# Up- and down-projection on eight named PSUM banks, two recombination steps at higher priority, and adding transfers behind the scaling

## The chip, the cores and the metric

The kernel runs as one program on 1 core of a Trainium2 chip. The metric is the time of one execution in microseconds on the device. Five engines work at the same time, each through its own instructions in order: TensorE (PE) multiplies matrices and writes into PSUM, VectorE (DVE), ScalarE (ACT) and GpSimd (POOL) do elementwise work, and SyncE (SP) issues most of the DMA transfers. An engine waits for another only by a semaphore on the instruction that needs it. PSUM, in which matmuls accumulate, is used here as eight banks, each of which holds one tile of 128 x 512 float32.

## The reference

One decoder layer on x of 1024 tokens by 1024 channels in float32. Cut to what matters:

```python
def conv_ffn(xn, w_up, conv_w, conv_b, w_down):
    u = xn @ w_up                                   # 1024 x 5632
    upad = jnp.pad(u, ((0, 0), (CONV_WIDTH - 1, 0), (0, 0)))
    c = conv_b
    for j in range(CONV_WIDTH):                     # CONV_WIDTH = 3
        c = c + upad[:, j:j + S] * conv_w[j]
    gate, val = jnp.split(c, 2, axis=-1)            # 2816 each
    return (jax.nn.silu(gate) * val) @ w_down

def reference(x, ...):
    xn = rmsnorm(x, norm_mix_w)
    da_q, da_k, da_v, sw_q, sw_k, sw_v, g_da, g_sw = split_cols(xn @ w_in)
    ...
    y_da = diff_attention(da_q, da_k, da_v, lam, lam_init, subln_w)
    y_sw = sliding_window_attention(sw_q, sw_k, sw_v, sinks)
    merged = sigmoid(g_da) * (y_da @ w_br_da) + sigmoid(g_sw) * (y_sw @ w_br_sw)
    x = x + merged @ w_mix_out
    x = x + conv_ffn(rmsnorm(x, norm_ffn_w), w_up, conv_w, conv_b, w_down)
    return rmsnorm(x, norm_final_w)
```

## The kernel before

The stages follow each other: the projection with w_in (up to about 235 us of the profiled execution), attention (to about 490 us), the gates and the mixing product (to about 664 us), the up-projection (`hidden`, to about 1093 us), the down-projection (`down`) with the final norm (from 1100 us to the end). Data lie transposed, channels over the 128 partitions and tokens along them, in two halves of 512 tokens.

The large products are made by the Strassen-Winograd scheme. A pair of output column blocks (128 channels each) over two halves of tokens is a 2 x 2 block matrix, and seven products P1 to P7 of sums and differences replace eight. Each operand is also split in a high part and a low part (`wh`, `wl` for weights, `sh`, `sl` for their sums), where ACT casts the high part and DVE subtracts it from the raw value to get the low one; three matmuls (high x high, high x low, low x high) stand for one. So a product is 12 matmuls of 128 x 128 by 512, and one pair is 84.

In the up-projection the loop runs over j = 0 to 21, and pair j is made of columns j and j + 22 of w_up (gate and value). PE makes the products of a pair in the order P1, P2, P5, P6, P7, P3, P4 (for the last pair P1, P2, P5, P6, P7, P4, P3), each into a tile of its own in PSUM. Around them, per pair:

- POOL makes the sums of weight blocks (lines 156 to 159: `sa`, `sb` from `raw` and `rv`), from which ACT casts `sh` and DVE makes `sl` (line 172).
- `recombine` makes the four blocks of the result from the seven products. ACT copies P1 into s1 (line 524). DVE then reads the other products out of PSUM: line 526 takes P2, line 527 takes P6 into u2, line 528 takes P7 into u3 = u2 with P7, lines 529 and 530 take P5, line 532 takes P3 and line 533 P4. A bank is free again when the steps that read it are done.
- `conv` and `glu` of the pair before (j - 1): POOL and DVE scale the two column tiles `us` (line 1254), ACT starts the convolution (line 1268), DVE does its other two taps (lines 1270 and 1271, once for each of the two tiles), ACT applies silu (line 1243), DVE multiplies gate and value (line 1246), and the result goes to DRAM (`hd`), from which the down-projection reads it again.

What sets the order: the code is written pair after pair, and a scheduler places each engine's instructions by priority and readiness on a model; `high_priority` moves what it encloses ahead by as many places, `issue_after` keeps an instruction behind another one. On the chip each engine's order is fixed.

PSUM: in `hidden` a pool `psF` of eight tiles hands a bank to each product as it is asked for. In `down` another pool `psD` has four tiles named `d` and four named `y`, on the same eight banks: a chain of accumulating products in `down` (one output block m) has one of them. The first chains are y with m = 0 to 3 on stage P1, each with k chunks 0 to 5: 18 matmuls each (line 1324), weights `wh` and `wl` of a chain made by lines 191 (ACT) and 193 (DVE) from a load of w_down (line 181). Their other operand, the high and low parts of `hd` tiles 0 to 5, is made at the end of `hidden` (lines 897 and 898, in tiles named `sh`, `sl`, `rv`).

In the projection, pairs of w_in columns go the same way, by the same `recombine`; afterwards POOL multiplies the two column tiles `us` by the norm factor (line 514). In that stage there also go transfers to DRAM that prepare sums of other weights for later stages (`presum`): a copy (line 126, issued by SP), and a transfer that adds to what is there (line 128, `accum_op`), which POOL issues, so that it stands in POOL's queue among its elementwise work. Their results, `md` and `ud`, are read by the mixing product and by the first pairs of the up-projection.

Of the kernel before, what the change touches and what calls it, by code (L numbers as in the profile page):

```python
# [17 lines left out]
P = 128  # L18
# [4 lines left out]
H2 = 512  # L23
# [26 lines left out]
class Trunk:  # L50
# [270 lines left out]
    def project(self):  # L321
# [6 lines left out]
        with ExitStack() as ctx:  # L328
# [170 lines left out]
            for j, ms in enumerate(self.pairs):  # L499
                w = self.next_w()  # L500
                for c in SUMS[j]:
                    with tc.issue_after(self.sync), tc.issue_after(self.sum):
                        self.presum(*c)
# [6 lines left out]
                for m, u in zip(ms, us):  # L510
                    if self.kind[m] == "g":
                        nc.sync.dma_start(self.gd[m - 18], u)
                    else:
                        nc.gpsimd.tensor_tensor(u, u, self.rstd, ALU.mult)
                        self.keep(m, u, (tp, "hi"))
        self.uw = None

    def recombine(self, ps, us, tp, o, after=None, pre=False):
# [8 lines left out]
        tt(u2, ps["P6"], s1, sub(pre))  # L527
        tt(u3, u2, ps["P7"], sub(pre))
# [571 lines left out]
    def hidden(self, w0):  # L1100
        nc, tc = self.nc, self.tc
        with self.hctx as ctx:
            e = ctx.enter_context
            psF = e(tc.tile_pool(name="psF", bufs=8, space=PSUM, reuse_waits="tile"))
            self.psT = psF
# [4 lines left out]
            for j in range(NF):  # L1110
                w, ps = ready.pop(j) if j else (w0, {})
                if j == 0:
# [8 lines left out]
                    ssq = self.tl(psF, [P, H2], "t")  # L1121
                    self.col_sums(ssq, [self.rstd[:, H2:]], 4, 4)
                    for i in (1, 6):
                        name, a, b = prods[i]
                        ps[name] = self.tl(psF, [P, H2], "t")
# [13 lines left out]
                for name, a, b in (prods[i] for i in ((0, 1, 2, 5, 3, 6, 4) if j == NF - 1 else (0, 1, 2, 5, 3, 4, 6) if j else range(7))):  # L1139
                    if name not in ps:  # L1140
                        ps[name] = self.tl(psF, [P, H2], "t")
# [13 lines left out]
                with nullcontext() if j else tc.issue_after(self.ms):  # L1155
                    self.recombine(ps, us, tp, 2, self.lo.ins if j == NF - 1 else None, j < NPRE)
                if j < NF - 1:
# [12 lines left out]
                    for name, a, b in prods[:2 if j == 0 else 0]:  # L1170
                        ps[name] = self.tl(psF, [P, H2], "t")
                        self.product(ps[name], w[a], b)
                if j == 0:
                    for hf in range(2):
                        sp = self.tl(psF, [P, H2], "t")
                        self.spread(sp, rs, hf * 4)
                        nc.scalar.copy(self.rstd[:, hf * H2:(hf + 1) * H2], sp)
                if j > NF - 3:
                    self.front = None

                self.us = us
                for w in range(2):
# [3 lines left out]
                    else:  # L1186
                        self.defer.append(f)

# [85 lines left out]
    def down(self):  # L1274

        nc, tc = self.nc, self.tc
        with ExitStack() as ctx:
            e = ctx.enter_context
            psD = self.psD = e(tc.tile_pool(name="psD", bufs=4, space=PSUM, reuse_waits="tile"))
# [4 lines left out]
            bank = lambda n: self.tl(psD, [P, H2], "dy"[n])  # L1284
# [60 lines left out]
            for stage in STAGES:  # L1345
                which, start, o, hf, done = plan[stage]
                for c in range(2):
                    for m in range(4):
# [5 lines left out]
                        if start and c == 0:  # L1354
                            chains[which][m] = bank(which)
# [156 lines left out]
```

## Time and profile before

| | us |
|---|---|
| median of 3 runs (lowest, highest) | 1326.28 (1325.94, 1328.66) |
| the profiled execution | 1327.68 |
| its span | 1325.7 |
| mean granted TensorE clock of it | 0.995 of full speed |
| PE busy, share of the span | 1302.1, 98% |
| DVE busy, share | 1075.4, 81% |
| ACT busy, share | 635.2, 48% |
| POOL busy, share | 498.0, 38% |

The profiled execution took 1.4 us more than the median, and 2.0 us of it lie outside its span. The shares are means over stages that differ: PE and DVE stand close to each other in the up-projection and far apart elsewhere. In the rows of the profile a group is named by line, engine, operation and tiles (out<-in), and an idle time is put down to the instruction that ended last of those waited for.

### The profile page before, as it was taken

The page shows a single profiled execution, that of the slowest core. Times are in us where ns is not written, and L with a number is a line of the kernel's source. Part 1 is how long each engine was busy: PE and PEld are TensorE (multiplying, and loading weights), DVE is VectorE, ACT ScalarE, POOL GpSimd, SP SyncE. Part 2 cuts the span into 40 slices and gives each one's busy share as a digit, 9 for nine tenths or more (in the row PEclk, how much of TensorE's full clock was granted, in tenths as well). Part 3 has the DMA queues.
Part 4 walks back from the last instruction along what each step waited for, and adds up shares of the span by engine and source line. Part 5 has one row for each costly group of instructions (what it writes and reads, how often), then busy time and mean ns, then how long its engine had stood idle before and what let it go on. Part 6 is the DMA issues. An engine that isn't in the chain of part 4 may idle for free.

```text
span 1325.7 us, 17315 instructions
## 1 busy us (share of the span) xinstructions
PE 1302.1 (98%) x6162; PEld 1081.6 (82%) x6162; DVE 1075.4 (81%) x1516; ACT 635.2 (48%) x1010; POOL 498.0 (38%) x399
## 2 busy tenths in 40 slices
PE   9999999999999999999999999999999997999997
PEld 7887888888888878888888788878888886888886
DVE  8835865289888977667899999999999997896865
ACT  9422232276667764335764343333434344554543
POOL 0456665000011015743327567766766632000002
PEclk9999999999999999999999999999999998999999
DMA  8366887876552256569763336554635227953534
GB/s 308 124 171 198 231 220 231 255 194 176 151 145 78 69 186 217 165 196 256 211 209 136 120 135 167 152 182 139 202 100 155 72 76 262 335 175 118 164 97 147
DMA packets 85510, 229.57 MB, mean 173 GB/s; under 512 B 9520, under 2 KB 17328, under 8 KB 85168
## 3 DMA queue, kind: packets, MB, share of 16 engines
q1 hardware_dynamic: 63328, 187.04, 42.5%
q0 software_dynamic: 9216, 24.12, 10.9%
q10 hardware_dynamic: 12880, 17.31, 3.7%
q8 instruction: 48, 0.79, 0.3%
q14 instruction: 38, 0.31, 0.1%
HBM read 173.39 MB, written 84.41 MB: 194 GB/s over the span
## 4 chain that ended last, share of the span: by engine, by line
PE 64%; DVE 17%; issue 9%; DMA 4%; POOL 4%; ACT 2%; SPq 0%; POOLq 0%; DVEq 0%; ACTq 0%
PE t L1097 13%; PE y L1324 9%; PE d L1324 7%; PE m L1059 6%; PE g L212 4%; PE g L213 4%; PE g L214 4%; DVE wl L172 3%; DVE c L1270 3%; PE sc L700 3%; DMA rv<-in_w_up 2%; DVE c L1271 2%; POOL sf L156 1%; DVE c L1246 1%; PE t L716 1%
## 5 line engine op out<-in xcount | busy, mean ns | idle before, releaser
L193 DVE TENSOR_TENSOR wl<-raw,wh 128x1024 fp32r<-128x1024 f32 (+2 forms) x91 | 109.7, 1207 | 52.5 <-ACT wh L191 42.7
L191 ACT CAST wh<-raw 128x1024 fp32r<-128x1024 f32 (+2 forms) x91 | 80.4, 885 | 105.5 <-PE y L1324 52.8
L1254 POOL TENSOR_TENSOR us<-us,rstd 128x1024 f32<-128x1024 f32 x42 | 93.5, 2301 | 57.3 <-DVE us L532 29.0
L1268 ACT ACTIVATE c<-us,vecs 128x1024 f32<-128x1024 f32 x44 | 54.7, 1247 | 114.0 <-POOL us L1254 109.9
L229 POOL TENSOR_TENSOR rs<-ms,mhalf 128x8 f32<-128x8 f32 (+2 forms) x9 | 13.3, 1476 | 236.4 <-DVE ms L227 230.2
L156 POOL TENSOR_TENSOR sf<-rv 128x512 f32<-128x512 f32 x29 | 59.8, 2061 | 104.6 <-DMA rv<-in_w_up 49.8
L172 DVE TENSOR_TENSOR sl<-sf,sh 128x1024 fp32r<-128x1024 f32 x58 | 74.0, 1276 | 10.8 <-ACT sh L170 10.7
L1097 PE MATMUL t<-x,wh 128*128 128x512 f32 x240 | 79.8, 390 | 0.0
L170 ACT CAST sh<-sf 128x1024 fp32r<-128x1024 f32 x58 | 60.0, 1042 | 39.2 <-POOL us L1253 19.7
L172 DVE TENSOR_TENSOR wl<-raw,wh 128x1024 fp32r<-128x1024 f32 x29 | 69.7, 2404 | 4.0 <-ACT wh L170 3.9
L1271 DVE SCALAR_TENSOR_TENSOR c<-us,vecs,c 128x1024 f32<-128x1024 f32 x44 | 72.7, 1685 | 0.1
L212 PE MATMUL g<-xh,wh 128*128 128x512 f32 x176 | 71.1, 404 | 0.9 <-ACT g L629 0.8
L1097 PE MATMUL t<-x,sh 128*128 128x512 f32 x220 | 70.8, 390 | 0.0
L214 PE MATMUL g<-xh,wl 128*128 128x512 f32 x176 | 70.5, 401 | 0.0
L213 PE MATMUL g<-x,wh 128*128 128x512 f32 x176 | 70.4, 400 | 0.0
L1270 DVE SCALAR_TENSOR_TENSOR c<-us,vecs,c 128x1024 f32<-128x1024 f32 x44 | 67.1, 1559 | 1.2 <-ACT c L1268 1.2
L158 POOL TENSOR_TENSOR sf<-raw,rv 128x512 f32<-128x512 f32 x29 | 53.1, 1830 | 34.4 <-DVE sl L172 34.4
L1324 PE MATMUL y<-h,wh 128*128 128x512 f32 (+1 forms) x224 | 65.3, 375 | 0.0
L704 DVE CUSTOM_DVE_ANT_0 L<-sc,bias 128x128 f32<-128x128 f32 (+7 forms) x64 | 47.8, 752 | 16.7 <-PE sc L700 13.7
L683 POOL MEMSET aT<- 128x128 f32 x32 | 6.1, 204 | 145.8 <-PE t L729 97.8
L1097 PE MATMUL t<-z,sh 128*128 128x512 f32 x176 | 55.7, 398 | 4.0 <-DVE u L527 4.0
L705 ACT ACTIVATE L<-L,sm 128x128 f32<-128x128 f32 (+7 forms) x64 | 49.6, 778 | 20.0 <-DVE sm L704 17.4
(350 smaller groups left out, 4097.1 us busy)
## 6 DMA issues: line engine op xcount, KB each, us to landing
u<-qd SPq DMA_DIRECT2D x70, 256.0 KB, 6.5
raw<-in_w_in SPq DMA_DIRECT2D x22, 512.0 KB, 6.3
raw<-in_w_up SPq DMA_DIRECT2D x22, 512.0 KB, 5.3
hd<-c SPq DMA_DIRECT2D x22, 512.0 KB, 2.6
sdP<-in_w_down POOLq DMA_DIRECT2D x16, 704.0 KB, 8.5
rv<-in_w_up SPq DMA_DIRECT2D x20, 512.0 KB, 3.7
hc<-hd SPq DMA_DIRECT2D x33, 256.0 KB, 4.8
gr<-gd SPq DMA_DIRECT2D x16, 512.0 KB, 4.4
```

The lines of the kernel that those rows point to most:

```text
L172: low = nc.vector.tensor_tensor(lo, src, hi.bitcast(F32), ALU.subtract)
L191: self.hi = nc.scalar.copy(wh, raw)
L193: self.lo = (eng or nc.vector).tensor_tensor(wl, raw, wh.bitcast(F32), ALU.subtract)
L212: nc.tensor.matmul(ps, wh[:, kc + o, :], ah, start=first and n == 0, stop=False)
L213: nc.tensor.matmul(ps, wh[:, kc + o, :], al, start=False, stop=False)
L214: nc.tensor.matmul(ps, wl[:, kc + o, :], ah, start=False, stop=last and n == len(kcs) - 1)
L1059: nc.tensor.matmul(ps, v[:, m % 2 * 4 + k, :], x, start=start and k == j == 0, stop=k == 3 and j == 2, skip_group_check=True)
L1097: nc.tensor.matmul(ps, (ah, ah, al)[p][:, k, :], (bh, bl, bh)[p], start=first and n == p == 0, stop=last and p == 2 and n == len(ks) - 1, ...
L1254: i = (nc.vector if m % NF == 0 else nc.gpsimd).tensor_tensor(us[:, 2:], us[:, 2:], self.rstd, ALU.mult)
L1270: nc.vector.scalar_tensor_tensor(c, us[:, 1:T + 1], cw[1], c, ALU.mult, ALU.add)
L1271: nc.vector.scalar_tensor_tensor(c, us[:, 0:T], cw[0], c, ALU.mult, ALU.add)
L1324: nc.tensor.matmul(ps, v[:, k - k0, :], x, start=start and k == i == 0, stop=k == HK - 1 and i == 2, skip_group_check=True)
```

## The change

There are three edits.

1. One PSUM pool, `psF`, is now used by `hidden` and `down`, with eight tiles that are named by number. A table (`banks`) says for each pair which product has which bank. From j = 2 on, P1 takes the bank that stood free, P2 the one that P1 had, P5 that of P2, P6 and P7 keep theirs, P3 takes that of P5 and P4 that of P3 (for the last pair P3 and P4 change places), and the bank of P4 becomes the free one. The chains of `down` then take fixed banks: y with m = 0 the free bank, m = 1 to 3 those of P1, P6 and P7 of the last pair; the d chains those of P2, P5, P4 and P3. `last_norm` gets its banks by name.
2. In `recombine` the steps u2 and u3 (before: lines 527 and 528) are put at a priority that is higher by 150 for the pairs 1 to 20 of the up-projection.
3. In the projection, the transfers of `presum` are put behind the scaling of the pair's last column tile instead of behind the weight sums.

```diff
@@ project
             for j, ms in enumerate(self.pairs):
                 w = self.next_w()
-                for c in SUMS[j]:
-                    with tc.issue_after(self.sync), tc.issue_after(self.sum):
-                        self.presum(*c)
...
                     else:
-                        nc.gpsimd.tensor_tensor(u, u, self.rstd, ALU.mult)
+                        last = nc.gpsimd.tensor_tensor(u, u, self.rstd, ALU.mult).ins
                         self.keep(m, u, (tp, "hi"))
+                for c in SUMS[j]:
+                    with tc.issue_after(self.sync), tc.issue_after(last):
+                        self.presum(*c)
@@ recombine
-        tt(u2, ps["P6"], s1, sub(pre))
-        tt(u3, u2, ps["P7"], sub(pre))
+        with self.tc.high_priority(early):
+            tt(u2, ps["P6"], s1, sub(pre))
+            tt(u3, u2, ps["P7"], sub(pre))
@@ hidden
-            psF = e(tc.tile_pool(name="psF", bufs=8, space=PSUM, reuse_waits="tile"))
-            self.psT = psF
+            self.psF = self.fctx.enter_context(tc.tile_pool(name="psF", bufs=1, space=PSUM, reuse_waits="tile"))
+            banks = dict(P1=0, P5=1, P3=2, P7=3, P6=4, P2=6, P4=7)
...
+                if j == 1:
+                    banks, free = dict(P1=0, P2=5, P5=1, P6=2, P7=7, P3=6, P4=4), 3
+                elif j:
+                    b = banks
+                    c, d = ("P4", "P3") if j == NF - 1 else ("P3", "P4")
+                    banks = {"P1": free, "P2": b["P1"], "P5": b["P2"], "P6": b["P6"], "P7": b["P7"], c: b["P5"], d: b["P3"]}
+                    free = b["P4"]
...
-                        ps[name] = self.tl(psF, [P, H2], "t")
+                        ps[name] = self.bank(banks[name])
...
-                    self.recombine(ps, us, tp, 2, self.lo.ins if j == NF - 1 else None, j < NPRE)
+                    self.recombine(ps, us, tp, 2, self.lo.ins if j == NF - 1 else None, j < NPRE, 150 if 0 < j < NF - 1 else 0)
...
+                if j == NF - 1:
+                    self.ybanks = [free] + [banks[n] for n in ("P1", "P6", "P7")]
+                    self.dbanks = [banks[n] for n in ("P2", "P5", "P4", "P3")]
...
+    def bank(self, n):
+        return self.tl(self.psF, [P, H2], f"t{n}")
@@ down
-            psD = self.psD = e(tc.tile_pool(name="psD", bufs=4, space=PSUM, reuse_waits="tile"))
...
-            bank = lambda n: self.tl(psD, [P, H2], "dy"[n])
...
-                            chains[which][m] = bank(which)
+                            chains[which][m] = self.bank((self.dbanks, self.ybanks)[which][m])
...
-    def last_norm(self, psD, sqs, x3, t0, a, b, pieces):
+    def last_norm(self, banks, sqs, x3, t0, a, b, pieces):
```

How the order of instructions changes is shown at three places. Numbers behind a tile's name tell copies apart; what stands in brackets is whom an instruction waits for.

**DVE, one pair in the middle of the up-projection.** `wl` is the low part of the next weights, `c` are the tiles of the convolution, `sl` the low part of weight sums, `u2` and `u3` the two steps of `recombine`, `t` a product in PSUM. Before:

```order
L172 TENSOR_TENSOR wl_1316_7550<-raw_1311_7538,wh_1315_7548 128x1024
L1270 SCALAR_TENSOR_TENSOR c_1323_7568<-us_1305_7524,vecs_80,c_1323_7568 128x1024
L1270 SCALAR_TENSOR_TENSOR c_1324_7574<-us_1306_7525,vecs_80,c_1324_7574 128x1024
L1271 SCALAR_TENSOR_TENSOR c_1323_7568<-us_1305_7524,vecs_80,c_1323_7568 128x1024
L1271 SCALAR_TENSOR_TENSOR c_1324_7574<-us_1306_7525,vecs_80,c_1324_7574 128x1024
L172 TENSOR_TENSOR sl_1320_7558<-sf_1314_7543,sh_1319_7556 128x1024
L1246 TENSOR_TENSOR c_1323_7568<-c_1323_7568,c_1324_7574 128x1024
L527 TENSOR_TENSOR u2_1335_7675<-t_1328_7620,s1_1334_7674 128x512
L528 TENSOR_TENSOR u3_1336_7676<-u2_1335_7675,t_1329_7633 128x512
```

After (lines 1284, 1285 and 1260 are lines 1270, 1271 and 1246 of before, and 528 to 530 are 527 to 529):

```order
L172 TENSOR_TENSOR wl_1316_7550<-raw_1311_7538,wh_1315_7548 128x1024
L1284 SCALAR_TENSOR_TENSOR c_1323_7568<-us_1305_7524,vecs_80,c_1323_7568 128x1024
L1284 SCALAR_TENSOR_TENSOR c_1324_7574<-us_1306_7525,vecs_80,c_1324_7574 128x1024
L1285 SCALAR_TENSOR_TENSOR c_1323_7568<-us_1305_7524,vecs_80,c_1323_7568 128x1024
L528 TENSOR_TENSOR u2_1335_7675<-t2_1328_7620,s1_1334_7674 128x512
L1285 SCALAR_TENSOR_TENSOR c_1324_7574<-us_1306_7525,vecs_80,c_1324_7574 128x1024
L172 TENSOR_TENSOR sl_1320_7558<-sf_1314_7543,sh_1319_7556 128x1024
L529 TENSOR_TENSOR u3_1336_7676<-u2_1335_7675,t7_1329_7633 128x512
L1260 TENSOR_TENSOR c_1323_7568<-c_1323_7568,c_1324_7574 128x1024
```

u2 has moved ahead of the second of the two last taps, and u3 ahead of the product of gate and value. This is so for j = 1 to 20; the last pair has the order of before.

**PE, from the last matmuls of the up-projection to the first of the down-projection.** `t_1710` (`t1_1710`) is the last product, P3 of j = 21; `y_1726` (`t6_1726`) is the first chain of `down`. Before:

```order
L1097 MATMUL t_1710_9725<-B22_3_5762,sh_1670_9476 128x512 x2
L1097 MATMUL t_1710_9725<-B22_3_5762,sl_1671_9478 128x512
L1324 MATMUL y_1726_9795<-sh_1698_9629,wh_1690_9606 128x512 [waits DVE_49,Activation_49]
L1324 MATMUL y_1726_9795<-sh_1698_9629,wh_1690_9606 128x512
L1324 MATMUL y_1726_9795<-sh_1698_9629,wl_1691_9608 128x512
L1324 MATMUL y_1726_9795<-sl_1699_9632,wh_1690_9606 128x512 x2
```

After:

```order
L1098 MATMUL t1_1710_9725<-B22_3_5762,sh_1670_9476 128x512 x2
L1098 MATMUL t1_1710_9725<-B22_3_5762,sl_1671_9478 128x512
L1336 MATMUL t6_1726_9791<-sh_1698_9629,wh_1690_9606 128x512 [waits Activation_49]
L1336 MATMUL t6_1726_9791<-sh_1698_9629,wh_1690_9606 128x512
L1336 MATMUL t6_1726_9791<-sh_1698_9629,wl_1691_9608 128x512 [waits DVE_49]
L1336 MATMUL t6_1726_9791<-sl_1699_9632,wh_1690_9606 128x512 x2
```

The matmuls and their order are the same. The first matmul of the chain waited for DVE and ACT, and waits for ACT alone now; the third, which reads `wl`, has a wait for DVE that it had no need of before. The chain's tile is bank 6, that of P4 of j = 20.

**POOL, in the projection, behind the weight sums of one pair.** `us` are the two column tiles, `sf` the weight sums, `ud` and `mdP5` the results of `presum`. Before:

```order
L158 TENSOR_TENSOR sf_129_939<-raw_126_934,rv_127_936 128x512
L159 TENSOR_TENSOR sf_129_939<-raw_126_934,sf_128_938 128x512
L128 DMA ud0_92<-in_w_up 128x512
L514 TENSOR_TENSOR us_120_913<-us_120_913,rstd_83 128x1024
L128 DMA ud1_93<-in_w_up 128x512
L156 TENSOR_TENSOR sf_154_1083<-rv_153_1081 128x512
```

After:

```order
L158 TENSOR_TENSOR sf_129_939<-raw_126_934,rv_127_936 128x512
L159 TENSOR_TENSOR sf_129_939<-raw_126_934,sf_128_938 128x512
L511 TENSOR_TENSOR us_120_907<-us_120_907,rstd_83 128x1024
L128 DMA mdP5_88<-in_w_mix 128x512 x4
L156 TENSOR_TENSOR sf_154_1083<-rv_153_1081 128x512
```

The scaling of the second column tile now follows the weight sums at once, and a pair's adding transfers follow behind it. The same holds for the other pairs, and those of the first pair are issued one pair later than before. On SP, the copies of `presum` move a place or two with them, and at the start of `down` some of the weight loads come a few places earlier among the loads of `hd`.

More of the change, by code (lines that the diff above doesn't have):

```diff
@@ L1124, in hidden @@
                         name, a, b = prods[i]
-                        ps[name] = self.tl(psF, [P, H2], "t")
+                        ps[name] = self.bank(banks[name])
                         self.product(ps[name], w[a], b)
@@ L1140, in hidden @@
                     if name not in ps:
-                        ps[name] = self.tl(psF, [P, H2], "t")
+                        ps[name] = self.bank(banks[name])
                         self.product(ps[name], w[a], b, low=name == "P1")
```

20 lines of the change are left out of this document (10 added, 10 removed).

## The prediction

> **What bounds the kernel now.** First the page's busy shares, then the chain of waits grouped for PE.
>
> ```profile
> PE 1302.1 (98%) x6162; PEld 1081.6 (82%) x6162; DVE 1075.4 (81%) x1516; ACT 635.2 (48%) x1010; POOL 498.0 (38%) x399
> ```
>
> ```profile
> PE y L1324 <- DVE us L532: 7.1, 1, 7.1
> PE t L1097 <- DVE u L527: 4.0, 5, 1.6
> PE t L1097 <- DVE wl L172: 0.8, 1, 0.8
> ```
>
> PE is the bound; 23.6 us of the span are not busy. Of the waits, three kinds touch the change: one of 7.1 us in which the first chain of the down-projection stands for line 532, five in which P6 stands for line 527, and one of 0.8 us for `wl` in the projection: 11.9 us together. Next, PE at the boundary of up and down, in order of time:
>
> ```profile
> 1093.01 0.39 PE L1097 MATMUL t<-B,sl 128*128 128x512 f32 x1
> 1100.51 1.19 PE L1324 MATMUL y<-sh,wh 128*128 128x512 f32 x2 [7.12 <-DVE us L532]
> 1104.49 0.82 PE L1324 MATMUL y<-rv,wh 128*128 128x512 f32 x2
> 1106.75 0.62 PE L1324 MATMUL y<-sh,wh 128*128 128x512 f32 x2
> 1110.83 0.62 PE L1324 MATMUL y<-sh,wh 128*128 128x512 f32 x2
> ```
>
> From 1106.75 to 1110.83 is one chain of 18 matmuls: 4.08 us, 0.227 each. The chain before it took 6.24 us, because its first nine matmuls (1100.51 to 1104.49) went at 0.44 each: the stop cost 7.12 us and then 9 x 0.215 = 1.9 us of slow matmuls. Last, the up-projection by windows, one pair each, from line 527 to line 527, under a row for 17 pairs:
>
> ```profile
> 734.21:1062.44 328.23, 325.11 (x1425) 266.74 (x1426) 322.12 (x273) 127.83 (x136) 217.24 (x153) 1.00 0.48 144
> 753.35:772.49 19.14, 19.14 (x86) 15.71 (x85) 19.00 (x17) 7.49 (x8) 11.73 (x9) 1.00 0.44 158
> 791.64:808.71 17.07, 17.07 (x77) 13.98 (x76) 16.93 (x18) 6.03 (x6) 12.04 (x8) 1.00 0.68 178
> 808.71:830.61 21.90, 21.90 (x98) 17.94 (x96) 20.83 (x17) 9.07 (x10) 16.53 (x14) 1.00 0.53 138
> ```
>
> The columns behind the time are PE, weight load, DVE, ACT and POOL. 84 matmuls at 0.227 are 19.04 us. DVE is busy for 19.00 of 19.14 us and over the 17 pairs for 98%; the mean pair takes 328.23 / 17 = 19.31. So in this stage DVE sets the pace, by 0.1 us in regular pairs and more in irregular ones (17.07 then 21.90, together 38.97 against 38.28 for two regular).
>
> **The change, part by part.** *Banks.* Within the up-projection the plan is the one the old pool arrived at (P6 and P7 in their own banks, the others in rotation), so nothing moves there. At the boundary the first chain no longer needs the bank of the last product. What is late next is read from DVE and ACT, whose order here stays:
>
> ```profile
> 1092.32 0.95 DVE L193 TENSOR_TENSOR wl<-raw,wh 128x768 fp32r<-128x768 f32 x1
> 1096.91 1.06 DVE L193 TENSOR_TENSOR wl<-raw,wh 128x768 fp32r<-128x768 f32 x1
> 1099.68 0.68 DVE L532 TENSOR_TENSOR us<-t,u 128x512 f32<-128x512 f32 x1
> 1100.28 1.27 DVE L1271 SCALAR_TENSOR_TENSOR c<-us,vecs,c 128x1024 f32<-128x1024 f32 x1
> 1107.59 0.96 DVE L193 TENSOR_TENSOR wl<-raw,wh 128x768 fp32r<-128x768 f32 x1 [6.04 <-ACT wh L191]
> ```
>
> ```profile
> 1097.19 1.24 ACT L1268 ACTIVATE c<-us,vecs 128x1024 f32<-128x1024 f32 x1 [2.53 <-POOL us L1254]
> 1106.72 0.84 ACT L191 CAST wh<-raw 128x768 fp32r<-128x768 f32 x1 [8.29 <-PE y L1324]
> ```
>
> On DVE's clock: chain 0 follows at 1093.24; its `wl` is done at 1093.27 and is read by the third matmul only, at 1093.7. It ends at 1097.32. Chain 1 reads its `wl` (done at 1097.97) in its third matmul, due at 1097.77: 0.2 late, so it ends at 1101.6. Chain 2 has its `wh` cast when chain 0 is read (1097.3), but ACT is in line 1268 until 1098.4: cast until 1099.3, in time. Its `wl` stands behind line 1271 (end 1101.55), so 1102.5 against 1102.05: 0.45 late. Chain 2 thus runs as if begun at 1102.05, where it began at 1110.83: **8.8 us** gained. The stops that are left are under half a microsecond; stops of up to 1.6 us in the up-projection (the waits above) left the granted clock at 1.00 in the windows above, so I count no slow matmuls.
>
> *Loads of the down-projection.* Does the rest follow 8.8 us earlier?
>
> ```profile
> 1099.78 9.13 SPq L181 DMA_DIRECT2D raw<-in_w_down  x2
> ```
>
> ```profile
> 1104.00:1109.00 5.00, 5.00 (x21) 4.05 (x20) 1.41 (x2) 1.88 (x3) 0.00 (x0) 0.91 0.03 13
> 1109.00:1165.00 56.00, 56.00 (x248) 46.39 (x247) 49.99 (x66) 31.83 (x49) 4.76 (x2) 1.00 0.96 327
> ```
>
> SP stands at the second of two loads until about 1108.6, when the `wl` of chain 2 has read its `raw`; DMA is idle (0.03) until then and afterwards 0.96 full for 56 us. That `wl` now ends at 1102.5 instead of 1108.55, so the loads begin 6.0 us earlier, 2.8 less than PE. PE never waited in those 56 us, so there is slack, of a size that the trace does not show. Bounds 0 and 2.8 us; I take 0.5, near the lower end, since no wait of PE stands there now.
>
> *u2 and u3 earlier.* No instruction is added; two move on DVE. DVE now, with POOL beside it:
>
> ```profile
> 766.79 3.51 DVE L1271 SCALAR_TENSOR_TENSOR c<-us,vecs,c 128x1024 f32<-128x1024 f32 x2
> 770.22 1.21 DVE L172 TENSOR_TENSOR sl<-sf,sh 128x1024 fp32r<-128x1024 f32 x1
> 771.36 1.21 DVE L1246 TENSOR_TENSOR c<-c,c 128x1024 f32<-128x1024 f32 x1
> 772.49 0.68 DVE L527 TENSOR_TENSOR u<-t,s 128x512 f32<-128x512 f32 x1
> 773.28 0.69 DVE L528 TENSOR_TENSOR u<-u,t 128x512 f32<-128x512 f32 x1
> 774.00 0.69 DVE L529 TENSOR_TENSOR us<-u,t 128x512 f32<-128x512 f32 x1
> 774.60 0.68 DVE L530 TENSOR_TENSOR u<-u,t 128x512 f32<-128x512 f32 x1
> ```
>
> ```profile
> 771.51 2.21 POOL L158 TENSOR_TENSOR sf<-raw,rv 128x512 f32<-128x512 f32 x1 [2.19 <-DVE sl L172]
> 773.68 1.30 POOL L159 TENSOR_TENSOR sf<-raw,sf 128x512 f32<-128x512 f32 x1
> ```
>
> Line 527, 528 and 529 hang on each other and start 0.79 and 0.72 apart where independent ones are 0.60 apart (529 and 530 do not hang on each other): spread out, that gives back 0.3 us a pair. Against it: line 158 runs 1.30 us when alone (as line 159 does), but 2.21 here, because it stood until line 1246 was done; both work on SBUF alone, while 527 to 530 read PSUM and were not slowed by POOL. Now u3 stands between `sl` and 1246. Line 158, released by `sl`, starts under u3 (0.6 us), and 1246 stands for the other 1.30 - 0.6 = 0.7 us. So a regular pair costs +0.7 - 0.3 = +0.4. The irregular pairs come from here:
>
> ```profile
> 804.04 2.47 DVE L1271 SCALAR_TENSOR_TENSOR c<-us,vecs,c 128x1024 f32<-128x1024 f32 x2
> 816.00 5.56 DVE L172 TENSOR_TENSOR wl<-raw,wh 128x1024 fp32r<-128x1024 f32 x1
> 805.37 4.57 POOL L156 TENSOR_TENSOR sf<-rv 128x512 f32<-128x512 f32 x1 [4.72 <-DMA rv<-in_w_up]
> ```
>
> `rv` landed late, line 156 then stood behind four DVE operations in a row until line 527, its successors piled up, and DVE's `wl` paid with 5.56 instead of 1.2 us. With u2 between the two runs of line 1271, POOL gets its turn earlier; I give each double pair -0.5, between nothing and -1.0 (its whole excess, 38.97 - 38.28 = 0.7, and 0.3 for the spacing). Of the 17 pairs, (328.23 - 17 x 19.14) / 0.7 = 4 are double, 9 regular; over the 20 pairs that is 10.6 regular and 4.7 double: 10.6 x 0.4 - 4.7 x 0.5 = **+1.9 us** on DVE, which PE follows. The 4.0 us of waits for line 527 are no gain of their own: u2 releases P6 some 3.5 us earlier (the rows of 1271, `sl` and 1246 above), but P4 then waits for the `wl` of A22, which DVE makes in the same lap.
>
> The Trainium skill (SBUF — State Buffer, Who interferes with whom) says that a DVE instruction with two SBUF inputs and a GpSimd instruction that reads SBUF share an exclusive lock, and whichever issues first holds it while the other fully blocks. By that rule 1246 pays the 0.7 us in every pair, as taken above; line 156 at 805.37, which stood while DVE started two more such operations, shows that the first to ask is not always the first to get it, and if DVE kept its turn here too, the sum would be -0.3 a pair, the third rival below.
>
> *Projection.* The scaling on POOL stood behind an adding transfer:
>
> ```profile
> 115.51 0.82 POOL L128 DMA_DIRECT2D ud<-in_w_up  x1
> 116.08 2.67 POOL L514 TENSOR_TENSOR us<-us,rstd 128x1024 f32<-128x1024 f32 x1
> 118.78 1.06 ACT L545 ACTIVATE hi<-us 128x1024 fp32r<-128x1024 f32 x1 [12.88 <-POOL us L514]
> ```
>
> The scaling now starts 116.08 - 115.51 = 0.57 us earlier; from it hang ACT's `hi`, the casts behind that, and the `wl` that PE waited 0.84 us for. Bounds 0 and 0.57, I take **0.4**. The transfers go out up to one pair later; their results are read from about 550 us on, which covers a delay of some 20 to 30 us; SP's copies hide behind its idle time.
>
> *Sum* against the profiled 1327.68: 8.8 + 0.4 - 0.5 - 1.9 = 6.8, so 1320.9; that execution is 1.4 over the median, so the median goes from 1326.28 to **1319.5**.
>
> **The rivals.** *Port (other side).* At the place of u3, POOL takes its turn twice (158 and then 159, another 1.30 us) before 1246: +0.7 + 1.3 - 0.3 = 1.7 a pair, 34 us over 20 pairs, 1326.3 - 8.7 + 34 = 1351.6. It speaks against this that POOL and DVE took turns between 766 and 770. With +0.4 in all 20 pairs and no gain from the irregular ones it is 8.0 us and 1325.6, no change. Slower by over 0.2% (2.65 us, about what a measurement of this kernel tells from no change) it gets from (8.7 + 2.65) / 20 = 0.57 us a pair.
>
> *Loads.* PE eats the lead and waits for the load queue, the stop moves some chains on: the full 2.8 instead of 0.5, 1321.8; if the double pairs also give nothing (2.3 us more on DVE), 1324.1.
>
> *DVE keeps its turn.* Pairs shrink by 0.3 and fall to PE's own 19.04: 20 x 0.27 = 5.4 gained instead of 1.9 lost, 1312.2.
>
> *The wait only changes its name.* If a `y` chain waits for a later reader of its bank, the 7.1 us come back. The readers of the banks it gets (P4 of pair 20, P1, P6, P7 of pair 21) stand ahead of line 532 on DVE, so this has little for it: 1326.
>
> **How the numbers follow.** The sum as worked out 0.57 (own range 1316.5 to 1322.5); port 0.19, of which no change 0.10, slower 0.06; loads 0.12, mostly faster; DVE keeps its turn 0.09; changed name 0.03. Faster by over 0.2% means under 1323.63. That gives 0.80 faster, 0.13 within, 0.07 slower. The range leaves out the far port case and the end of the DVE case: 1314.0 to 1325.2.
>
> **What would show it.** Right: no stop over 1 us between the last product of up and chain 2 of down, 0.227 us from the first chain on, the granted clock at 1.00 there, line 1246 (now 1260) about 1.9 instead of 1.21 us in regular pairs, line 158 near 1.30, pairs of 19.4 to 19.5 us. Wrong: pairs above 19.8 us or at 19.04, or new PE waits for loads between 1100 and 1165.

## The result, and the profile after

The changed kernel took 1323.30 us in the median of 14 runs (1321.97 to 1326.55), the kernel before, beside it, 1327.28 us (1325.73 to 1328.79). The ratio is 0.9973, with a 95% interval of 0.9964 to 0.9981: faster by 0.27%, some 3.6 us, where 6.8 us were forecast. The profiled execution of the changed kernel took 1322.11 us (span 1320.3), 1.2 below its median.

First the busy shares and the grouped waits of PE, as they were shown of before.

```profile
PE 1301.6 (99%) x6162; PEld 1081.8 (82%) x6162; DVE 1081.6 (82%) x1516; ACT 636.3 (48%) x1010; POOL 501.8 (38%) x399
```

```profile
PE t L1336 <- DVE wl L193: 2.4, 2, 2.2
PE t L1098 <- DVE us L526: 2.4, 1, 2.4
PE t L1098 <- DVE wl L172: 2.2, 3, 1.3
```

The three kinds of waits that the change was aimed at are gone: the 7.1 us for line 532, the five for u2, the one in the projection. Three others stand in their place, 7.0 us together. In order of time they are, with the matmuls by which PE's position is compared with before:

```profile
121.69 0.39 PE L1098 MATMUL t<-xh,wl 128*128 128x512 f32 x1
...
713.42 1.22 PE L1098 MATMUL t<-T,sh 128*128 128x512 f32 x2 [2.36 <-DVE us L526]
...
1088.43 0.50 PE L1098 MATMUL t<-T,wl 128*128 128x512 f32 x1 [1.32 <-DVE wl L172]
...
1093.33 0.39 PE L1098 MATMUL t<-B,sl 128*128 128x512 f32 x1
1093.55 0.62 PE L1336 MATMUL t<-sh,wh 128*128 128x512 f32 x2
...
1098.44 0.50 PE L1336 MATMUL t<-sh,wl 128*128 128x512 f32 x1 [0.19 <-DVE wl L193]
...
1102.21 0.61 PE L1336 MATMUL t<-sh,wh 128*128 128x512 f32 x2
...
1106.67 0.62 PE L1336 MATMUL t<-sh,wh 128*128 128x512 f32 x2
...
1120.38 0.50 PE L1336 MATMUL t<-x,wl 128*128 128x512 f32 x1 [2.21 <-DVE wl L193]
```

Before, in the same order of matmuls, these stood elsewhere:

```profile
122.89 0.50 PE L1097 MATMUL t<-xh,wl 128*128 128x512 f32 x1 [0.84 <-DVE wl L172]
...
1126.24 0.39 PE L1324 MATMUL y<-x,wl 128*128 128x512 f32 x1
```

With the rows of the prediction this gives the account of the two profiled executions:

| up to | before | after | after minus before | added by the stretch |
|---|---|---|---|---|
| the matmul of the old stop in the projection | 122.89 | 121.69 | -1.2 | -1.2 |
| last matmul of the up-projection (attention and mixing lie between) | 1093.01 | 1093.33 | +0.3 | +1.5 |
| first matmul of chain 2 of the down-projection | 1110.83 | 1102.21 | -8.6 | -8.9 |
| the third matmul of chain 6 | 1126.24 | 1120.38 | -5.9 | +2.8 |
| the span | 1325.7 | 1320.3 | -5.4 | +0.5 |

So the boundary gave what was forecast, and of the 10.1 us that were gained (1.2 and 8.9) nearly half was given back, mostly in two places: in the up-projection, and some 25 us behind the boundary. Of the 1.5 us of the second row 0.6 were lost ahead of the up-projection: the matmul at 642.97 us before came at 642.40.

**Behind the boundary.** DVE and SP of the changed kernel there:

```profile
1113.69 3.09 DVE L899 TENSOR_TENSOR x<-hc,x 128x512 fp32r<-128x512 f32 x2
1118.90 0.69 DVE L1342 TENSOR_TENSOR x<-x,t 128x512 f32<-128x512 f32 x1 [2.12 <-DMA x<-x2d]
1119.51 0.82 DVE L193 TENSOR_TENSOR wl<-raw,wh 128x640 fp32r<-128x640 f32 x1
```

```profile
1111.42 0.89 SPq L1374 DMA_DIRECT2D x<-x2d  x2
```

and before:

```profile
1124.31 0.69 DVE L1330 TENSOR_TENSOR x<-x,y 128x512 f32<-128x512 f32 x1 [0.66 <-DMA x<-x2d]
1124.92 0.82 DVE L193 TENSOR_TENSOR wl<-raw,wh 128x640 fp32r<-128x640 f32 x1
```

```profile
1119.18 0.89 SPq L1362 DMA_DIRECT2D x<-x2d  x2
```

Line 1342 (1330 before) is the first eviction: it adds a finished chain to the residual x, which is loaded from DRAM (`x2d`). On DVE it stands ahead of the `wl` of chain 6. SP issued the load just behind the end of chain 3: at 1119.18 before, when it had waited 1.4 us for PE, and at 1111.42 now, 0.5 us behind that end, because it was still at the loads of `hc`. That is 7.8 us earlier. The load let the eviction start at 1124.3 before and at 1118.9 now, only 5.4 earlier: 7.5 us behind its issue instead of 5.1. While the load was on its way the DMA moved 312 GB/s before (0.99 full) and 313 now (0.92 full): it was no slower, but it moved 2.3 MB in that time instead of 1.6. That the load stood behind more of the other transfers is likely; no experiment shows it. Before, the eviction waited 0.66 us, and the `wl` behind it was done at 1125.74, 0.5 us before the matmul at 1126.24 read it. Now the eviction waits 2.12 us, and PE 2.21.

**In the up-projection.** A regular pair, its DVE steps and POOL's beside them:

```profile
768.28:787.82 19.54, 19.54 (x88) 16.19 (x87) 19.54 (x17) 7.48 (x8) 11.93 (x8) 1.00 0.24 81
```

```profile
770.07 1.21 DVE L172 TENSOR_TENSOR sl<-sf,sh 128x1024 fp32r<-128x1024 f32 x1
771.21 0.68 DVE L529 TENSOR_TENSOR u<-u,t 128x512 f32<-128x512 f32 x1
771.80 1.94 DVE L1260 TENSOR_TENSOR c<-c,c 128x1024 f32<-128x1024 f32 x1
773.66 0.67 DVE L530 TENSOR_TENSOR us<-u,t 128x512 f32<-128x512 f32 x1
```

```profile
771.36 1.30 POOL L158 TENSOR_TENSOR sf<-raw,rv 128x512 f32<-128x512 f32 x1 [2.79 <-DVE sl L172]
772.62 2.28 POOL L159 TENSOR_TENSOR sf<-raw,sf 128x512 f32<-128x512 f32 x1
```

Line 158 has its turn under u3 (line 529) and takes 1.30 us, line 1260 stands for it and takes 1.94, and the pair takes 19.54 us instead of 19.14, each as forecast. The stop of 2.4 us at 713.42 was not: in pair 1 the higher priority put u2 and u3 ahead of line 526 too, which frees P2's bank for the third product of pair 2. It starts at 712.69 now:

```profile
704.63 0.68 DVE L528 TENSOR_TENSOR u<-t,s 128x512 f32<-128x512 f32 x1
...
708.01 0.67 DVE L529 TENSOR_TENSOR u<-u,t 128x512 f32<-128x512 f32 x1
...
712.69 0.68 DVE L526 TENSOR_TENSOR us<-s,t 128x512 f32<-128x512 f32 x1
```

and before it started 6.9 us earlier:

```profile
705.80 0.68 DVE L526 TENSOR_TENSOR us<-s,t 128x512 f32<-128x512 f32 x1
```

### The profile page after: what moved, and what is told of

It reads as the page before. It is cut to its first block, busy times and chain, and to the rows that moved or that the text cites. A ratio compares the mean times of both kernels' runs of the same rounds, so it can differ in the third digit from the quotient of the medians.

```text
span 1320.3 us, 17292 instructions
## 1 busy us (share of the span) xinstructions
PE 1301.6 (99%) x6162; PEld 1081.8 (82%) x6162; DVE 1081.6 (82%) x1516; ACT 636.3 (48%) x1010; POOL 501.8 (38%) x399
## 4 chain that ended last, share of the span: by engine, by line
PE 72%; DVE 13%; issue 6%; DMA 3%; POOL 3%; ACT 2%; SPq 0%; POOLq 0%; DVEq 0%; ACTq 0%
PE t L1098 23%; PE t L1336 14%; PE m L1060 6%; PE g L212 4%; PE g L213 4%; PE g L214 4%; PE sc L701 3%; DVE wl L172 2%; DVE c L1284 2%; DVE c L1285 2%; PE t L717 1%; DMA rv<-in_w_up 1%; PE sc L214 1%; PE sc L213 1%; PE sc L212 1%
## 5 line engine op out<-in xcount | busy, mean ns | idle before, releaser
L1336 PE MATMUL t<-h,wh 128*128 128x512 f32 (+1 forms) x360 | 107.2, 380 | 0.0
L156 POOL TENSOR_TENSOR sf<-rv 128x512 f32<-128x512 f32 x29 | 56.2, 1940 | 93.5 <-DMA rv<-in_w_up 43.1
L172 DVE TENSOR_TENSOR sl<-sf,sh 128x1024 fp32r<-128x1024 f32 x58 | 80.6, 1390 | 12.0 <-ACT sh L170 12.0
L1336 PEld LDWEIGHTS t<-h,wh 128*128 128x128 f32 x360 | 66.5, 188 | 12.8
L1336 PE MATMUL t<-x,wh 128*128 128x512 f32 (+1 forms) x228 | 69.6, 386 | 0.0
L1336 PE MATMUL t<-h,wl 128*128 128x512 f32 (+1 forms) x180 | 68.4, 380 | 0.0
L172 DVE TENSOR_TENSOR wl<-raw,wh 128x1024 fp32r<-128x1024 f32 x29 | 63.4, 2185 | 3.4 <-ACT wh L170 3.3
```

Source lines behind the costliest of these rows:

```text
L172: low = nc.vector.tensor_tensor(lo, src, hi.bitcast(F32), ALU.subtract)
L1336: nc.tensor.matmul(ps, v[:, k - k0, :], x, start=start and k == i == 0, stop=k == HK - 1 and i == 2, skip_group_check=True)
```

## The experiments

The theory after this reading: the boundary gave its 8.9 us; the moved steps cost on DVE, the x2d load costs a stop, and the stop in pair 2 costs nothing since PE waits for DVE at the end of the stage anyhow. In each experiment the kernel before ran beside the others on the same chip; ratios are to it. The changed kernel's own is 0.9973 (0.9964 to 0.9981).

**The first eviction later (e1).** The changed kernel, with

```diff
-                        for f in owed:
-                            f()
-                        owed = []
+                        if i != 5:
+                            with tc.issue_after(self.lo.ins) if i == 6 else nullcontext():
+                                for f in owed:
+                                    f()
+                            owed = []
```

and `owed` added to instead of replaced.

> The changed kernel, but in the down-projection the first eviction (the one that needs the x2d load) stands behind the weight casts of the next two chains on VectorE. Theory (late loads): the 2.2 us for which PE stood at wl after 1100 us in the changed kernel hang on this x2d load alone, so the stop goes and the time falls by 2.0 to 2.8 us against the changed kernel, to about 1320.7. Rival (DMA as a whole is late, whichever instruction meets it first): the stop moves to a load of w_down or hd a few chains on, and the time stays within 0.7 us of the changed kernel.

Ratio 0.9965 (0.9952 to 0.9977), median 1321.71. In the profile the wait for the `wl` of chain 6 is gone, and no other came behind it; DVE, where the eviction has moved to 1123.88:

```profile
1114.42 3.09 DVE L899 TENSOR_TENSOR x<-hc,x 128x512 fp32r<-128x512 f32 x2
1117.43 0.81 DVE L193 TENSOR_TENSOR wl<-raw,wh 128x640 fp32r<-128x640 f32 x1
...
1123.88 0.68 DVE L1342 TENSOR_TENSOR x<-x,t 128x512 f32<-128x512 f32 x1
```

In the profile the stop hangs on this one load, which the theory said; the third matmul of chain 6 came 2.4 us earlier against those ahead of it. Of that the whole shows 1.1 us, by the ratios as by the profiled spans (1319.2 against 1320.3), below the 2.0 forecast and above the rival's 0.7; the intervals allow either. In this profiled execution the up-projection took 1.3 us more than in the changed kernel's (table below).

**Pair 1 in its old place (e2).**

```diff
-  150 if 0 < j < NF - 1 else 0)
+  150 if 1 < j < NF - 1 else 0)
```

> The changed kernel, but u2 and u3 keep their old place in pair 1 (moved only in pairs 2 to 20), so that line 526 of pair 1 comes before them again. Theory (VectorE sets the end of the up-projection): the 2.4 us stop of PE at the third product of pair 2 and the slow matmuls behind it go, but the last pairs then wait for wl of A22 instead, and the time stays within 0.8 us of the changed kernel. Rival (the stop in pair 2 is where the gain went): 3.5 to 4.3 us faster than the changed kernel, about 1319.4.

Ratio 0.9961 (0.9948 to 0.9973), median 1321.58. The stop at 713 and the slow matmuls behind it are gone, which put PE 4.2 us ahead there. The waits at the `wl` of A22 took nearly all of it back:

```profile
PE t L1098 <- DVE wl L172: 3.4, 6, 1.3
PE t L1336 <- DVE wl L193: 2.2, 2, 2.0
```

Six instead of three, and the profiled spans differ by 0.5 us (1319.8 against 1320.3). By the ratios it is 1.6 us, more than the theory's 0.8, with intervals that allow nothing as well as about 3.5. The 3.5 to 4.3 of the rival are not seen: most of the stop was covered by the later waits, and it is not where most of the gain went.

**No moved steps (e3).**

```diff
-  150 if 0 < j < NF - 1 else 0)
+  0)
```

> The changed kernel without the higher priority of u2 and u3: banks and transfers changed, VectorE in the order of before. Theory (the moved steps cost VectorE 0.4 us in a regular pair and give a little back in double ones): the five stops at u2 come back, the stops at wl of A22 and the one in pair 2 go, regular pairs take 19.14 us again, and the time is 0.5 to 1.5 us below the changed kernel. Rival (the freed bank of P6 was worth its 4.0 us): 2 to 4 us slower than the changed kernel.

Ratio 0.9942 (0.9927 to 0.9957), median 1318.54: 4.1 us faster than the changed kernel by the ratios, where I expected 0.5 to 1.5. The direction was the theory's, the size was not; of the stops at u2 three came back (2.5 us), not five. From line 526 of pair 2 to u2 of the last pair, which stands at the same place in all kernels, DVE took 1090.43 - 721.23 = 369.2 us here:

```profile
721.23 0.68 DVE L526 TENSOR_TENSOR us<-s,t 128x512 f32<-128x512 f32 x1
...
1090.43 0.68 DVE L528 TENSOR_TENSOR u<-t,s 128x512 f32<-128x512 f32 x1
```

and 1093.62 - 721.18 = 372.4 in the changed kernel. The same stretch in every profiled execution with the product of gate and value:

| order of DVE | us |
|---|---|
| u2, u3 in their old place: before; e3, e6, e7, e9, e12 | 371.0; 369.2, 368.4, 369.3, 369.3, 368.6 |
| u2 and u3 moved: changed; e11, e1, e2, e8, e4 | 372.4; 372.6, 373.8, 372.3, 371.9, 373.0 |
| u2 alone moved: e5 | 370.8 |

The means are 369.3 and 372.7. The moved steps cost 3.4 us, and the profiled execution of before was the longest of its kind, 2.1 above the mean of the other five (368.9); against these five the cost is 3.7. In the profiled executions (spans 1315.8 and 1320.3) the rest of e3's gain is the x2d stop, which was 1.0 here instead of 2.2.

**The first chain on the bank of the last product (e4).**

```diff
-  self.ybanks = [free] + [banks[n] for n in ("P1", "P6", "P7")]
-  self.dbanks = [banks[n] for n in ("P2", "P5", "P4", "P3")]
+  self.ybanks = [banks[n] for n in ("P3", "P1", "P6", "P7")]
+  self.dbanks = [banks[n] for n in ("P2", "P5", "P4")] + [free]
```

> The changed kernel, but the first chain of the down-projection takes the bank of the last product P3 again and the free bank goes to the last d chain. Theory: the stop at the boundary comes back with about 7 us and 1.9 us of slow matmuls behind it, the waits for wl of chains 1 and 2 (0.6 us) and the one behind the x2d load (2.2 us) go, so 5.5 to 6.5 us slower than the changed kernel, about 1329. Rival (the boundary gave little, the gain came from the up-projection): less than 3 us slower.

Ratio 1.0012 (1.0000 to 1.0024), median 1327.64: 5.2 us slower than the changed kernel by the ratios. That is less than the 5.5 to 6.5 expected and more than the rival's 3. The experiment is not as clean as it was meant to be: the scheduler then put the beginning of chain 1 ahead of chain 0, so the stop came in two pieces, for the weights of chain 1:

```profile
1095.21 0.73 PE L1336 MATMUL t<-sh,wh 128*128 128x512 f32 x2 [1.42 <-ACT wh L191]
1098.53 0.80 PE L1336 MATMUL t<-sh,wl 128*128 128x512 f32 x1 [2.58 <-DVE wl L193]
```

with slow matmuls behind them. So it shows that the free bank for the first chain carries the gain at the boundary; it does not bring back the wait of 7.1 us as it was.

**u2 alone moved (e5).** Only `tt(u2, ...)` stays under the higher priority, from pair 2 on.

```diff
         with self.tc.high_priority(early):
             tt(u2, ps["P6"], s1, sub(pre))
-            tt(u3, u2, ps["P7"], sub(pre))
+        tt(u3, u2, ps["P7"], sub(pre))
```

> The changed kernel, but only u2 is moved (pairs 2 to 20), u3 stays behind the product of gate and value. Theory (the cost of the moved steps is u3: POOL's line 158 takes the SBUF turn under it and the product waits): line 1260 is back at 1.21 us, line 158 back at 2.2, regular pairs fall from 19.55 to 18.9 to 19.1 us, PE's stops at u2 do not come back, and the kernel is 4 to 6 us faster than the changed one, as fast as the one without any moved step or faster. Rival (it is u2 that costs, by cutting the two taps apart): regular pairs stay above 19.3 us.

Ratio 0.9970 (0.9959 to 0.9980), median 1321.62: no faster than the changed kernel, nor than e2, from which it differs by u3 alone. Line 1260 is back at 1.21 us and line 158 at 2.21, as the theory said, but regular pairs take 19.4 us, which is the rival's number. Not by cutting the two taps apart, though:

```profile
771.77 1.21 DVE L1260 TENSOR_TENSOR c<-c,c 128x1024 f32<-128x1024 f32 x1
772.90 0.68 DVE L529 TENSOR_TENSOR u<-u,t 128x512 f32<-128x512 f32 x1
773.61 0.69 DVE L530 TENSOR_TENSOR us<-u,t 128x512 f32<-128x512 f32 x1
774.22 0.68 DVE L531 TENSOR_TENSOR u<-u,t 128x512 f32<-128x512 f32 x1
774.81 1.65 DVE L172 TENSOR_TENSOR sl<-sf,sh 128x1024 fp32r<-128x1024 f32 x1
```

```profile
771.92 2.21 POOL L158 TENSOR_TENSOR sf<-raw,rv 128x512 f32<-128x512 f32 x1 [2.26 <-DVE sl L172]
774.09 1.29 POOL L159 TENSOR_TENSOR sf<-raw,sf 128x512 f32<-128x512 f32 x1
```

Now it is `sl` that pays, 1.65 instead of 1.22 us. In the old order four steps that read PSUM stand in a row (2.6 us or so), and POOL's lines 158 and 159 (1.30 each) fit under them. With u2 taken out, what is left is shorter than POOL's two operations, and the DVE operation behind it stands. So my theory, that u3 is the cost, was too narrow: by the table u2 alone costs 1.9 us (370.8 against 368.9), about half. Against e2 the stretch was 1.5 us shorter; a stop of 1.2 us in attention and a longer one behind the x2d load (2.6 instead of 2.0) took that back.

**Both losses taken out (e6), and again beside the changed kernel (e11, e12).** e6 and e12 are the same kernel: e3 with the eviction of e1. e11 is the changed kernel.

> Neither step moved, and the first eviction of the down-projection behind the weights of the next two chains. Theory: the two gains add up, 1.0 to 1.5 us less than without the moved steps alone (1318.5), since the stop behind the x2d load was 1.0 us there. Rival (DMA as a whole is late): no faster than 1318.5.

> The changed kernel once more, beside the one below on one chip. Theory: the stop behind the x2d load (about 2 us) and the pairs of 19.55 us stand in a second profiled execution as they did in the first; 3 to 5 us faster than before.

> The changed kernel with u2 and u3 in their old place and the first eviction behind the weights of the next two chains (as in e6), beside the changed kernel. Theory: the two losses found, 3 to 4 us from the moved steps and 1 to 2 us from the stop behind the x2d load, are both gone: 4 to 6 us faster than the changed kernel and 8 to 9 us faster than before. Rival (the losses overlap, one hides behind the other): 2 to 4 us faster than the changed kernel.

e6: ratio 0.9940 (0.9926 to 0.9955), median 1317.71. e11: 0.9969 (0.9956 to 0.9981), 1323.08. e12: 0.9928 (0.9912 to 0.9943), 1316.83. On the same chip e12 is 6.2 us below e11 in the medians and 5.4 by the ratios, and 9.5 us below the kernel before: the theory's numbers or a little more, where the two losses add up, and above the rival's 2 to 4. The eviction's own part of it (e6 against e3) is 0.3 us by the ratios, and the medians do not resolve it. The profiled spans differ by 2.3, but only 1.2 of that came at chain 6; 1.5 had come in the up-projection, where the two kernels are the same. What is left of PE's waits in e12 from the up-projection on:

```profile
PE t L1098 <- DVE u L528: 1.8, 1, 1.8
PE t L235 <- POOL rs L229: 1.1, 1, 1.1
PE t L220 <- ACT c L1324: 0.8, 1, 0.8
PE t L1336 <- DVE wl L193: 0.4, 1, 0.4
```

In e11 the wait of DVE for the x2d load was 1.50 us and PE's 1.6; the stop in pair 2 (2.7 us), the waits at the `wl` of A22 (2.6 us) and the pairs of 19.54 us were there as in the first profiled execution. The granted clock of e11's execution reads 0.95 in all stages and its matmuls are 0.227 us apart as elsewhere, so that reading did not cost it time.

**Each part alone (e7, e8, e9).** e7 is e3 with the transfers back in their place:

```diff
                 w = self.next_w()
+                for c in SUMS[j]:
+                    with tc.issue_after(self.sync), tc.issue_after(self.sum):
+                        self.presum(*c)
...
-                for c in SUMS[j]:
-                    with tc.issue_after(self.sync), tc.issue_after(last):
-                        self.presum(*c)
```

e8 is the kernel before with the edit of u2 and u3 alone, e9 the kernel before with the edit of the transfers alone:

```diff
+        with self.tc.high_priority(early):
             tt(u2, ps["P6"], s1, sub(pre))
             tt(u3, u2, ps["P7"], sub(pre))
```

```diff
-                for c in SUMS[j]:
-                    with tc.issue_after(self.sync), tc.issue_after(self.sum):
-                        self.presum(*c)
...
+                for c in SUMS[j]:
+                    with tc.issue_after(self.sync), tc.issue_after(last):
+                        self.presum(*c)
```

> The kernel before with the new bank plan alone: no moved steps, the adding transfers where they were. Theory (the banks carry the whole gain): 6 to 8.5 us faster than before, and 0.4 to 1.0 us slower than without the moved steps but with the moved transfers. Rival (the transfers' move also set the loads of the up-projection in better phase): less than 5 us faster than before.

> The kernel before with u2 and u3 moved in pairs 1 to 20 and nothing else. Theory: regular pairs 19.55 us, VectorE reaches the boundary 1 to 3 us later than before, the first chain of the down-projection waits for the last product as before, so 1 to 3 us slower than before. Rival (P6's bank freed earlier is worth its 4.0 us): 2 to 4 us faster than before.

> The kernel before with the adding transfers of the projection put behind the scaling and nothing else. Theory (POOL runs ahead of the transfers, the stop of PE at 122.9 us and the small one before it go): PE is 1.0 to 1.5 us earlier from there on, and the whole 0.5 to 1.5 us faster, since VectorE sets the pace of the up-projection only from its own start. Rival (the wait at the boundary or the up-projection eats it): within 0.3 us of before.

| | ratio | interval | us |
|---|---|---|---|
| e7, banks | 0.9960 | 0.9946 to 0.9974 | -5.3 |
| e8, u2 and u3 | 1.0026 | 1.0016 to 1.0035 | +3.4 |
| e9, transfers | 1.0002 | 0.9992 to 1.0012 | +0.3 |

The banks carry the gain, a little below what the theory said and just above the rival's bound; the interval, 3.4 to 7.2 us, does not part the two. The profiled spans differ by 8.3 us (1325.7 and 1317.4): 8.7 at the boundary and 1.6 ahead of it, where the profiled execution of before was long, less 2.0 behind the boundary, 1.7 of it at the stop behind the x2d load. The moved steps alone cost 3.4 us, a little more than the 1 to 3 expected; the wait of 7.2 us at the boundary stands there as before, and DVE's waits at the `wl` of A22 have come:

```profile
PE y L1325 <- DVE us L533: 7.2, 1, 7.2
PE t L1098 <- DVE wl L172: 3.7, 7, 1.3
```

The transfers alone brought nothing that can be measured, though PE was 1.0 us earlier at 121.93, where the stop was gone. The profiled execution of e9 had a stop of 1.92 us in attention that hangs on nothing the profile shows; the same matmul stopped PE for 1.1 or 1.2 us in e5, e10 and e11 and not in the others. Beside e3, which differs from it by the transfers alone, e7 is slower by 2.4 us by the ratios and 1.6 by the profiled spans, and its PE was 1.6 us later already at 185 us. So a gain of a microsecond or so from the transfers is likely on top of the banks, but the intervals of e3 and e7 overlap, and it stays open.

**Without the product of gate and value (e10).** Line 1260 left out of the changed kernel.

```diff
-            nc.vector.tensor_tensor(c0, c0, c, ALU.mult)
             nc.sync.dma_start(self.hd[j], c0)
```

> The changed kernel without the product of gate and value on VectorE (line 1260 left out, so silu of the gate alone goes on to the down-projection). PE does the same work. Theory (VectorE sets the pace of the up-projection): without its 1.14 us, or 1.86 with the wait, pairs fall to PE's own 19.04 to 19.1 us, the stops at wl of A22 go, and the time falls by 4 to 7 us against the changed kernel. Rival (PE is the bound of the stage and only stops at single places count): less than 2.2 us, the stops of the changed kernel at wl of A22.

Ratio 0.9932 (0.9913 to 0.9950), median 1316.85: 5.4 us faster than the changed kernel by the ratios. The waits at the `wl` of A22 and for the `wl` of chain 6 are gone; one is left:

```profile
PE t L1098 <- DVE us L526: 3.3, 1, 3.3
```

But PE was no earlier than in the changed kernel until 1030 us, and then gained 3.1 us at the `wl` of A22 in the last pairs, 0.9 at chains 1 and 2, and 2.3 at chain 6. So "VectorE sets the pace" is true of the end of the stage only: up to there the changed kernel's PE ran at its own 19.04 us a pair, making up for the stop in pair 2, and met DVE's clock in the last pairs.

## Why the prediction was right and wrong

- *Banks, 8.8 us.* Right, and term by term: 8.9 up to the first matmul of chain 2 and 8.6 with its wait for `wl` behind that. The first chain began 0.22 us behind the last product and at 0.227 us a matmul; chains 1 and 2 met their `wl` about as worked out (0.19 us late at 1098.44; chain 2 took 4.46 us, 1102.21 to 1106.67, where 4.08 is the rule).
- *Loads of the down-projection, 0.5 us.* Here the prediction failed first: of the bounds 0 and 2.8 it took 0.5, and the upper one came. Chain 6 lost 2.4 us (2.8 in the table, less the 0.4 of chain 2), and 0.4 more went to the end. A PE wait behind a load at 1120, which I had named as a sign of being wrong, stood there. I took the lower end because no wait of PE stood there before. One of DVE did, 0.66 us for the x2d load, ahead of a `wl` that was 0.5 us in time: the slack was 0.5 us. PE was due there 8.2 us earlier, the eviction started 5.4 earlier, and the rest less the slack is 2.3. The bounds were set by another load, that of w_down; the one that stopped PE was x2d. e1 and e12 show in their profiles that it is this load and this eviction. The size differs between executions: the wait is 2.2 us here, 1.6 in e11, 1.0 in e3.
- *u2 and u3, 1.9 us.* The mechanism was right (1260 at 1.94, 158 at 1.30, pairs of 19.54), and against the profiled execution of before even the size (1.4 us). Over all executions the term is 3.4 us (the table under e3, and e8 alone), so this is the second term that was too small. That PE follows DVE held in the changed kernel in the last pairs only (e10). The double pairs, which I counted as a gain of 0.5 each, differ from execution to execution; the one that I had was 2.1 us longer than the others of its order, and a change that is weighed against it looks better than it is. e5 shows that not u3's place alone mattered, but that steps were taken out of the row of four that read PSUM.
- *u2 releases P6, no gain of its own.* Right: the waits for u2 went, those at the `wl` of A22 came (2.2 us), and e8 is slower, not faster.
- *Pair 1* was not foreseen. I took pairs 1 to 20 to be alike; in pair 1 line 526 stood between and came 6.9 us later. It stopped PE for 2.4 us with some slow matmuls behind it, and by e2 cost 0.5 us (spans) to 1.6 (ratios). The sum had no term for it.
- *Projection, 0.4 us.* Under-sized in the trace: 1.2 us. I moved the scaling past one transfer, 0.57 us; it started 7.3 us earlier (108.75 against 116.08), since the transfers ahead of the weight sums had gone too, and the stop went whole. Alone it did not show in the time (e9).
- *The sum.* 6.8 was forecast; 5.4 is the difference of the profiled spans, 4.0 that of the medians and 3.6 the one by the ratio. The profiled execution of before lay 0.4 above the median of its 14 runs, that of the changed kernel 1.2 below its own: of the 5.6 us by which these two executions differ, 1.6 are in the choice of the executions, not in the change. With the terms as measured the sum is 8.6 + 1.2 - 2.8 - 3.4 = 3.6. That it meets the ratio to a tenth is luck, since the last three differ by about a microsecond between executions.
- *Rivals.* "Loads" came true in mechanism and nearly in size (1321.8; 1324.1 with the double pairs giving nothing), though it had only 0.12. "Port" was there with its first half, 0.4 us a pair, and not with its second: POOL and DVE took turns, and line 1260 never stood for both of POOL's operations (1.95 us at most in the changed kernel and e2). "DVE keeps its turn" and "the wait only changes its name" did not happen.

The Trainium skill (SBUF — State Buffer, Who interferes with whom) has the later of two operations stand until the first is done, where one is VectorE's with two SBUF inputs and the other GpSimd's that reads SBUF. Line 1260 at 771.80 and `sl` at 774.81 in e5 agree with it: each ended 1.08 us behind the end of the POOL operation beside it (1.94 and 1.65 us in all).

## What to carry to other kernels

When a change takes away a long stop, look along the path behind it for waits that were small and harmless, on any engine: an engine that waited 0.66 us for a load leaves little slack behind it (0.5 us here), and what starts 8 us earlier will ask for that load 8 us earlier. Where another engine's work fits under a row of steps, as POOL's 2.6 us did here under the four that read PSUM, count what the row still covers when one or two of its steps leave it. And weigh a term of a few microseconds against several executions: here one differed from the next by 2 us in a single stage.

## What the hardware showed that I had not expected

A short stop can have slow matmuls behind it. In the changed kernel 2.36 us at 713.42 were followed by matmuls 0.43 us apart (the granted clock from 712 to 718 us was 0.72), and in e12 even 1.83 us:

```profile
733.97 0.73 PE L1098 MATMUL t<-z,sh 128*128 128x512 f32 x2 [1.83 <-DVE u L528]
734.54 0.47 PE L1098 MATMUL t<-z,sl 128*128 128x512 f32 x1
734.81 1.05 PE L1098 MATMUL t<-z,sh 128*128 128x512 f32 x2
735.66 0.63 PE L1098 MATMUL t<-z,sl 128*128 128x512 f32 x1
```

The first three go at the usual distance or nearly so, the next at 0.43 us each (0.85 for two): the slowing comes some 0.8 us behind the stop. In the changed kernel 2.21 us at 1120.38 were followed by none, and in e11, the same kernel again, the stop in pair 2 was longer, 2.7 us, and was followed by none. So the length of the stop alone does not decide. The Trainium skill (TensorE: Matmul & The Clock Gate, What's actually happening) gives an idle window of about 3.4 us for the slow clock; it also says that the window is free-running, which would make the phase count, but here stops of 1.83 and 2.36 us already had slow matmuls behind them.
